# Gate chunks of a ConvFFN by seven block products, with deferred epilogues and a second sum of squares

## Chip, core and metric

One core of a Trainium2 chip runs the whole program in one launch. The metric is device time in microseconds: the median of repeated runs, with the lowest and the highest beside it. One further run is profiled, and all rows below come from that one execution.

## What is computed

A small two-layer decoder trunk (model width 1024; 544 tokens, 512 of a prompt and 32 of samples, in two halves of 272 columns). Layer 0 is RMSNorm, a gated recurrent block, and a ConvFFN; layer 1 is shared K/V, dilated attention, and a second ConvFFN. The change lies nearly all in the two ConvFFNs, and a little in the first RMSNorm:

```python
D_MODEL, D_FF = 1024, 3072
def rmsnorm(x, g):
    return x * lax.rsqrt(jnp.mean(x * x, axis=-1, keepdims=True) + EPS) * g

def causal_dwconv(prev, x, w, b):                  # width 3 here
    xc = jnp.concatenate([prev, x], axis=1)
    return b + sum(xc[:, j:j + T] * w[j] for j in range(3)), xc[:, T:]

def conv_ffn(h, prev, w_up, conv_w, conv_b, w_down):
    g, v = jnp.split(h @ w_up, 2, axis=-1)         # gates and values, 3072 each
    gc, new_prev = causal_dwconv(prev, g, conv_w, conv_b)
    return (jax.nn.gelu(gc) * v) @ w_down, new_prev

x = x + conv_ffn(rmsnorm(x, g_f), ...)
```

## The kernel before

**Layout.** Activations lie transposed: a tile of 128 channels by 2 halves of 272 tokens. `X[0..7]` is the residual stream. A matmul works on an fp32 operand split into a high part (`hh`, `HH`, weights' `hi`) and a remainder (`hl`, `HL`, `lo`); each product of a 128x128 weight block with 272 columns is three matmuls: hi·hi, hi·lo, lo·hi (`step3`, L192). An output chunk of 128 channels over 8 input chunks and 2 halves is 48 matmuls; a pair of chunks is 96.

**Weights.** They come in units of 512 KB into `raw` (three buffers). A unit is split into two `w` tiles (eight buffers): ScalarE (ACT) copies the high part (L131, L142, L163, 128x1024 each; L148, 128x512), VectorE (DVE) subtracts it (L132, L143, L164, L149). `conv_more(room)` issues these as far ahead as `w` tiles are to be had, in the order of the list `items`; `use()` calls it before each new weight.

**Seven block products.** A pair of value chunks (`duo`, `product`, L485) is not made as 96 matmuls. The weight blocks and the token halves form 2x2 block matrices, and seven products of 12 matmuls each give the four results, with sums of weights (DVE, 128x512 each: L155, L156, L158, L159) and of inputs (`T12`, `T34`, made once per layer) as operands: 84 matmuls. The products accumulate in one-bank PSUM tiles (`bank`). ACT copies partial results out (`snap`, L490; L585), DVE adds them (L587) into `cr` in SBUF.

**Order in an FFN.** There are 24 gate chunks and 24 value chunks, in six groups j of four. In each group: four gate chunks, each `full_job` (48 matmuls into a two-bank PSUM tile `big`), after each of them `g_done`; then `down(j-1)`, eight output chunks o of 24 matmuls each (two `big` tiles in turn), each added into `X[o]` by DVE (L610); then two value pairs, after each of them `v_done`. The sixth `down` stands behind the loop. So from group 1 on one round of the loop is 192 + 192 + 168 = 552 matmuls, and there are five such rounds in each of two FFNs.

`g_done` works on a gate chunk: DVE multiplies it by `rstd` into `E` (L532, L534), ACT and DVE do the width-3 convolution (L540, L541, L543, L546), ACT the gelu (L549), and GpSimd (POOL) multiplies by `rstd` once more (L550). `v_done` multiplies value and gate (DVE L553) and splits the result into `HH` and `HL` (ACT L295, DVE L296).

**PSUM.** `psum_pools(bigs, banks)` closes the PSUM pools and opens new ones: three `big` and two `bank` outside the FFN loops, two and four inside. A tile of a new pool waits for the readers of what lay at its place.

**The first norm.** While the inputs arrive, squares of `X[k]` are made on ACT (odd k, L262) or DVE (even k, L264) into two buffers `sqx`; POOL adds seven of them into `ss` (L266). `total` sums over partitions by a matmul with ones (L271), in the midst of the first three output chunks, and makes `rstd` from it.

**Order of instructions.** TensorE (PE) takes its matmuls in the order written. For the other engines a scheduler decides the order within a window; each engine then works in that order.

Of the kernel before, what the change touches and what calls it, by code (L numbers as in the profile page):

```python
# [14 lines left out]
P = 128  # L15
# [30 lines left out]
def trunk_kernel(ctx, tc, wall, xin, par_d, cst_d, msk_d, rope_d, bmask_d, ckT_d, cv_d,  # L46
# [20 lines left out]
    def psum_pools(bigs, banks):  # L67

        if psum:
            psum["ctx"].close()  # L70
        psum["ctx"] = ExitStack()
        for name, n in (("pp", bigs), ("aux", banks)):
            psum["n"] = psum.get("n", 0) + 1
            psum[name] = psum["ctx"].enter_context(pool(f"{name}{psum['n']}", n, space=bass.MemoryType.PSUM))
# [14 lines left out]
    def ffn_items(b0):  # L89
        def up(kind, j, i):  # L90
            return b0 + (0 if j == 0 else 12 * j - 4) + 4 * kind + i

        def duo(kind, j, i):
            return [("a", n, up(kind, j, i), up(kind, j, i + 1)) for n in range(4)]

        def down(j):
            return [("u", b0 + (16 + 12 * j if j < 5 else 68) + q) for q in range(4)]

        order = []
        for j in range(6):  # L100
            order += [("u", up(0, j, i)) for i in range(4)] + (down(j - 1) if j else []) + duo(1, j, 0) + duo(1, j, 2)
        return order + down(5)
# [77 lines left out]
    def use(held=0):  # L180

        conv_more(WBUFS - held)
        i = nxt["use"]
        nxt["use"] += 1
        return split.pop(items[i][1] if items[i][0] == "u" else i)
# [56 lines left out]
    class Norm:  # L242
# [12 lines left out]

        def square(self, k, on_act=True):
            if k == 0:
                sq = self.ss = self.hp.tile([P, 2, T], F32, name="ss", tag="ss", bufs=1)
            else:
                sq = self.hp.tile([P, 2, T], F32, name="sqx", tag="sqx", bufs=2)  # L260
            if on_act:
                ACT.activation(sq, X[k], AF.Square)  # L262
            else:
                DVE.tensor_tensor(sq, X[k], X[k], op=ALU.mult)  # L264
            if k:
                POOL.tensor_tensor(self.ss, self.ss, sq, op=ALU.add)  # L266

        def total(self):
            ps = [bank(), bank()]
            for h in range(2):  # L270
                PE.matmul(ps[h][:, :T], lhsT=ones, rhs=self.ss[:, h, :], start=True, stop=True)  # L271
            tc.keep_in_program_order(ACT.preload_act_table_set("natural_log_exp_and_others"))
# [148 lines left out]
    for k in range(KC):  # L421
        if k in (0, 4):
            for u in range(3):
                conv(u, k * P, k * P + HALF)
        nrm.gain(k, pcol("g_a", k))
        nrm.square(k, on_act=k % 2 == 1)
    first = [(split.pop(u), big()) for u in range(3)]
# [36 lines left out]

    def product(form, snap, done):

# [26 lines left out]
        prod(0, A, True)  # L493
        s1 = keep(A)
        prod(1, G, True)
        p5 = keep(G)
        prod(2, A, False)
        u2 = keep(A)
        B = bank()[:, :T]
        prod(3, B, True)  # L500
        done(0, 0, (s1, B))
        prod(4, A, False)
        done(1, 1, (p5, keep(A)))
        prod(5, G, False)
        done(0, 1, (u2, G))
        prod(6, A, False)
        done(1, 0, (A,))

    def ffn(layer, nrm, hpool, fctx, ectx, after):
# [4 lines left out]
        fo = fp.tile([P, FC, 18], F32, name="fo")  # L514
        psum_pools(2, 4)
        E = [fp.tile([P, 562], F32, name=f"E{i}") for i in range(2)]
# [10 lines left out]
        def g_done(c, src):  # L527
# [46 lines left out]
        def form(n, k, part):  # L574
            x0, x1 = nrm.x(2 * k)[part], nrm.x(2 * k + 1)[part]
            t12, t34 = T12[k][part], (T34h, T34l)[part][k]
            return {0: x0[:, 0], 1: t12[:, 0], 2: t12[:, 1], 3: x1[:, 0], 4: t34[:, 0], 5: x1[:, 1], 6: t34[:, 1]}[n]

        def duo(c):
# [9 lines left out]
            product(form, snap, done)  # L589
            return t  # L590

        def gates(j):
            for c in range(4 * j, 4 * j + 4):
                g_done(c, full_job(nrm.x))

        def values(c):
            for i, t in enumerate(duo(c)):
                v_done(c + i, t)

# [4 lines left out]
        def down(j):  # L604
            for q in range(4):
                w = use()
                for o in (2 * q, 2 * q + 1):
                    ps = big()
                    down_part(o, ps, w, j, range(4))
                    DVE.tensor_tensor(X[o], X[o], ps[:, :, :T], op=ALU.add)  # L610

        def down_last():
# [25 lines left out]
        for c in (2, 3):  # L638
            g_done(c, full_job(nrm.x))
        for j in range(6):  # L640
            if j:
                gates(j)
                down(j - 1)
            values(4 * j)
            values(4 * j + 2)
        SP.dma_start(ffn_d[:, layer], fo)
        ectx.close()
# [664 lines left out]
```

## Time and profile before

| | |
|---|---|
| median of 3 runs | 1324.05 us (1323.76 to 1325.4) |
| profiled execution | 1323.6 us |
| its span, first to last instruction | 1321.8 us |
| mean granted TensorE clock over the span | 0.988 |
| PE busy / DVE / ACT / POOL | 96% / 70% / 48% / 19% of the span |

The span is what all the rows below divide up; 1.8 us of the profiled execution lie outside of it. Busy shares are means over stages that are unlike: the stretches in which PE is not busy lie at the start, between the parts, and in attention.

### The profile page before, as it was taken

The page shows a single profiled execution, that of the slowest core. Times are in us where ns is not written, and L with a number is a line of the kernel's source. Part 1 is how long each engine was busy: PE and PEld are TensorE (multiplying, and loading weights), DVE is VectorE, ACT ScalarE, POOL GpSimd, SP SyncE. Part 2 cuts the span into 40 slices and gives each one's busy share as a digit, 9 for nine tenths or more (in the row PEclk, how much of TensorE's full clock was granted, in tenths as well). Part 3 has the DMA queues.
Part 4 walks back from the last instruction along what each step waited for, and adds up shares of the span by engine and source line. Part 5 has one row for each costly group of instructions (what it writes and reads, how often), then busy time and mean ns, then how long its engine had stood idle before and what let it go on. Part 6 is the DMA issues. An engine that isn't in the chain of part 4 may idle for free.

```text
span 1321.8 us, 24032 instructions
## 1 busy us (share of the span) xinstructions
PE 1272.7 (96%) x9853; PEld 1239.3 (94%) x9853; DVE 923.1 (70%) x1429; ACT 628.6 (48%) x1047; POOL 249.8 (19%) x284
## 2 busy tenths in 40 slices
PE   6999989999999999999999998798999999999998
PEld 6999989999999999999999787488999999999998
DVE  7986769766766666667877445779776666666763
ACT  5768646525353434445545255256535343434431
POOL 4464333010101010104114221033110101010100
PEclk8999999999999999999999999898999999999999
DMA  6232221314132322323255252311313232222312
GB/s 204 81 97 97 84 80 33 128 65 128 64 113 81 111 82 89 103 76 140 73 155 173 72 198 104 116 65 33 128 65 112 80 112 81 90 96 74 116 64 84
DMA packets 42174, 130.45 MB, mean 99 GB/s; under 512 B 7792, under 2 KB 8304, under 8 KB 41616
## 3 DMA queue, kind: packets, MB, share of 16 engines
q1 hardware_dynamic: 42064, 128.92, 29.3%
q8 instruction: 77, 1.26, 0.4%
q14 instruction: 33, 0.27, 0.1%
HBM read 119.99 MB, written 8.39 MB: 97 GB/s over the span
## 4 chain that ended last, share of the span: by engine, by line
PE 82%; DVE 10%; ACT 4%; issue 2%; DMA 1%; POOL 0%; SPq 0%; DVEq 0%; ACTq 0%; POOLq 0%
PE big L192 54%; PE bank L485 19%; PE big L881 2%; PE big L817 2%; DVE w L132 1%; PE big L867 1%; ACT w L131 1%; DVE hl L253 1%; DVE cc L358 1%; PE big L962 1%; PE big L714 1%; PE big L930 1%; DMA X<-in_xin 1%; PE bank L1059 0%; PE bank L817 0%
## 5 line engine op out<-in xcount | busy, mean ns | idle before, releaser
L192 PE MATMUL big<-hh,w 128*128 128x272 f32 x2560 | 439.9, 292 | 19.1 <-ACT hh L252 5.9
L192 PEld LDWEIGHTS big<-hh,w 128*128 128x128 f32 x2560 | 368.6, 191 | 20.5 <-ACT hh L252 5.9
L192 PE MATMUL big<-hl,w 128*128 128x272 f32 x1280 | 269.0, 291 | 1.7 <-DVE hl L253 1.6
L192 PE MATMUL big<-HH,w 128*128 128x272 f32 x1536 | 257.2, 288 | 1.0 <-ACT cr L585 1.0
L131 ACT ACTIVATE w<-raw 128x1024 fp32r<-128x1024 f32 (+1 forms) x151 | 156.9, 1039 | 163.5 <-PE big L192 130.6
L192 PEld LDWEIGHTS big<-HH,w 128*128 128x128 f32 x1536 | 217.4, 188 | 1.4 <-ACT cr L585 1.4
L132 DVE TENSOR_TENSOR w<-raw,w 128x1024 fp32r<-128x1024 f32 (+1 forms) x151 | 189.5, 1256 | 29.7 <-PE bank L485 18.8
L192 PEld LDWEIGHTS big<-hl,w 128*128 128x128 f32 x1280 | 203.8, 191 | 2.9 <-DVE hl L253 2.9
L550 POOL TENSOR_TENSOR G<-G,rstd 128x544 f32<-128x544 f32 x48 | 72.4, 1511 | 626.6 <-ACT G L549 626.6
L192 PE MATMUL big<-HL,w 128*128 128x272 f32 x768 | 159.2, 288 | 0.0
L192 PEld LDWEIGHTS big<-HL,w 128*128 128x128 f32 x768 | 120.6, 188 | 0.0
L485 PE MATMUL bank<-hh,w 128*128 128x272 f32 x576 | 119.8, 288 | 0.0
L610 DVE TENSOR_TENSOR X<-X,big 128x544 f32<-128x544 f32 x80 | 57.3, 717 | 64.7 <-PE big L192 64.7
L163 ACT ACTIVATE w<-sum 128x1024 fp32r<-128x1024 f32 x48 | 50.7, 1059 | 104.0 <-PE big L192 102.4
L485 PEld LDWEIGHTS bank<-hh,w 128*128 128x128 f32 x576 | 94.8, 188 | 0.0
L485 PE MATMUL bank<-hl,w 128*128 128x272 f32 x288 | 82.8, 288 | 0.0
L485 PE MATMUL bank<-t34h,w 128*128 128x272 f32 x384 | 80.0, 288 | 0.0
L532 DVE TENSOR_TENSOR E<-big,rstd 128x512 f32<-128x512 f32 x48 | 33.1, 689 | 65.4 <-PE big L192 65.2
L485 PE MATMUL bank<-t12h,w 128*128 128x272 f32 x384 | 76.0, 287 | 0.0
L549 ACT ACTIVATE G<-G 128x544 f32<-128x544 f32 x48 | 31.7, 659 | 93.1 <-DVE G L546 52.2
L266 POOL TENSOR_TENSOR ss<-ss,sqx 128x544 f32<-128x544 f32 x28 | 48.2, 1723 | 115.6 <-ACT sqx L262 112.0
L164 DVE TENSOR_TENSOR w<-sum,w 128x1024 fp32r<-128x1024 f32 x48 | 59.3, 1235 | 12.3 <-PE bank L485 8.8
(266 smaller groups left out, 2099.8 us busy)
## 6 DMA issues: line engine op xcount, KB each, us to landing
raw<-in_wall SPq DMA_DIRECT2D x193, 512.0 KB, 3.5
ck<-in_ckT SPq DMA_DIRECT2D x8, 512.0 KB, 6.3
X<-in_xin SPq DMA_DIRECT2D x8, 272.0 KB, 6.3
out_y<-X SPq DMA_DIRECT2D x8, 272.0 KB, 2.1
cv<-in_cv SPq DMA_DIRECT2D x8, 256.0 KB, 4.1
cvt<-in_cv SPq DMA_DIRECT2D x4, 512.0 KB, 4.2
raw<-in_wall SPq DMA_DIRECT2D x6, 256.0 KB, 5.7
out_kT<-KT SPq DMA_DIRECT2D x1, 1088.0 KB, 5.2
```

Of the source, the lines that this page charges most:

```text
L131: ACT.activation(hi[:, c0:c1], st, AF.Copy)
L132: DVE.tensor_tensor(lo[:, c0:c1], st, hi[:, c0:c1].bitcast(F32), op=ALU.subtract)
L163: ACT.activation(hi, flat, AF.Copy)
L164: DVE.tensor_tensor(lo, flat, hi.bitcast(F32), op=ALU.subtract)
L192: PE.matmul(ps[:, h, :T], lhsT=w[wi], rhs=x[xi][:, h, :], start=first and wi == 0 and xi == 0, stop=last and wi == 1)
L266: POOL.tensor_tensor(self.ss, self.ss, sq, op=ALU.add)
L485: PE.matmul(dst, lhsT=w, rhs=form(n, k, xi), start=first and k == 0 and wi == 0 and xi == 0, stop=k == 3 and wi == 1, skip_group_check=True)
L532: DVE.tensor_tensor(e[:, 2:514].rearrange("p (h t) -> p h t", h=2), prompt(src), prompt(nrm.rstd), op=ALU.mult)
L549: ACT.activation(g, g, AF.Gelu_apprx_tanh)
L550: POOL.tensor_tensor(g, g, nrm.rstd, op=ALU.mult)
L610: DVE.tensor_tensor(X[o], X[o], ps[:, :, :T], op=ALU.add)
L817: PE.matmul(o, lhsT=l, rhs=w[wi][:, 512 * kk:512 * kk + 512], start=k == 0 and wi == 0 and xi == 0, stop=k == KC - 1 and wi == 1)
```

## The change

1. The gate chunks of groups 1 to 5 are made by the seven block products too (`gates_of`, `duo`), with the list `items` altered to match; those of group 0 stay as they are.
2. `g_done` and `v_done` of a pair are put into a list `posts` and traced inside the next `product` (two places) or behind the first two output chunks of `down`. `product` also calls `conv_more` at fixed places with a fixed room.
3. The multiplication of the gelu by `rstd` goes from POOL to DVE.
4. `psum_pools(2, 4)` moves from the start of `ffn` to behind group 0's four gate chunks, and the two pools are laid out in the other order.
5. In the first norm odd squares from k = 3 on are added into a second sum `ss2` by DVE; POOL keeps the even ones. `total` multiplies both with ones.

```diff
         for j in range(6):
-            order += [("u", up(0, j, i)) for i in range(4)] + (down(j - 1) if j else []) + duo(1, j, 0) + duo(1, j, 2)
+            order += duo(0, j, 0) + duo(0, j, 2) + down(j - 1) if j else [("u", up(0, j, i)) for i in range(4)]
+            order += duo(1, j, 0) + duo(1, j, 2)
...
-            if k:
+            if two and k > 1 and k % 2:
+                DVE.tensor_tensor(self.ss2, self.ss2, sq, op=ALU.add)
+            elif k and sq is not self.ss2:
                 POOL.tensor_tensor(self.ss, self.ss, sq, op=ALU.add)
...
-                PE.matmul(ps[h][:, :T], lhsT=ones, rhs=self.ss[:, h, :], start=True, stop=True)
+                for x in (self.ss, self.ss2):
+                    if x is not None:
+                        PE.matmul(ps[h][:, :T], lhsT=ones, rhs=x[:, h, :], start=x is self.ss,
+                                  stop=x is self.ss2 or self.ss2 is None)
...
         prod(1, G, True)
         p5 = keep(G)
+        conv_more(WBUFS - 4)
         prod(2, A, False)
         u2 = keep(A)
+        if posts:
+            posts.pop(0)()
+        conv_more(WBUFS - 2)
         B = bank()[:, :T]
         prod(3, B, True)
         done(0, 0, (s1, B))
+        conv_more(WBUFS)
         prod(4, A, False)
         done(1, 1, (p5, keep(A)))
+        if posts:
+            posts.pop(0)()
+        conv_more(WBUFS - 2)
...
-        psum_pools(2, 4)
...
-            POOL.tensor_tensor(g, g, nrm.rstd, op=ALU.mult)
+            DVE.tensor_tensor(g, g, nrm.rstd, op=ALU.mult)
...
-        def gates(j):
-            for c in range(4 * j, 4 * j + 4):
-                g_done(c, full_job(nrm.x))
+        def gates_of(c):
+            t = duo(c)
+            posts.extend([lambda i=i: g_done(c + i, t[i]) for i in range(2)])
...
                     DVE.tensor_tensor(X[o], X[o], ps[:, :, :T], op=ALU.add)
+                    if posts:
+                        posts.pop(0)()
...
+        psum_pools(2, 4)
         for j in range(6):
             if j:
-                gates(j)
+                gates_of(4 * j)
+                gates_of(4 * j + 2)
                 down(j - 1)
```

**PE, where group 1's gates end and its `down` begins.** Before, the gates write `big` tiles with pairs of matmuls for the two halves:

```order
L192 MATMUL big<-hl,w 128x272 x2
L192 MATMUL big<-hh,w 128x272 x2
L192 MATMUL big<-HH,w 128x272 x2
L192 MATMUL big<-HL,w 128x272 x2
L192 MATMUL big<-HH,w 128x272 x4
```

Now the gates end with a product into a `bank` tile, from the sums of inputs:

```order
L497 MATMUL bank<-t34l,w 128x272
L497 MATMUL bank<-t34h,w 128x272 x2
L497 MATMUL bank<-t34l,w 128x272
L497 MATMUL bank<-t34h,w 128x272
L194 MATMUL big<-HH,w 128x272 x2
L194 MATMUL big<-HL,w 128x272 x2
```

What follows in `down` is the same; what moved is the kind and the number of the matmuls ahead of it.

**DVE, around the start of `down` in a round.** The names `X_77`, `X_81`, `X_85`, `X_88` are the residual tiles 0 to 3; `E_2283`, `E_2284` the two conv buffers. Before (L610 adds an output chunk into `X`):

```order
L132 TENSOR_TENSOR w<-raw,w 128x1024
L541 SCALAR_TENSOR_TENSOR cc<-E_2291,par,cc 128x560
L610 TENSOR_TENSOR X_77<-X_77,big 128x544
L543 SCALAR_TENSOR_TENSOR G<-E_2291,par,cc 128x2x256
L546 SCALAR_TENSOR_TENSOR G<-E_2291,par,cc 128x2x16
L156 TENSOR_TENSOR sum<-sum,raw 128x512
L530 COPY E_2291<-par 128x8x2
L159 TENSOR_TENSOR sum<-raw,sum 128x512
L610 TENSOR_TENSOR X_81<-X_81,big 128x544
L143 TENSOR_TENSOR w<-raw,w 128x1024
L610 TENSOR_TENSOR X_85<-X_85,big 128x544
```

Now, from the last weight split of the gates on (L638 is the same add):

```order
L133 TENSOR_TENSOR w<-raw,w 128x1024
L552 COPY E_2283<-par 128x8x2
L554 TENSOR_TENSOR E_2283<-cr,rstd 128x512
L638 TENSOR_TENSOR X_77<-X_77,big 128x544
L556 TENSOR_TENSOR E_2283<-cr,rstd 128x8x4
L552 COPY E_2284<-par 128x8x2
L554 TENSOR_TENSOR E_2284<-cr,rstd 128x512
L556 TENSOR_TENSOR E_2284<-cr,rstd 128x8x4
L156 TENSOR_TENSOR sum<-raw 128x512
L563 SCALAR_TENSOR_TENSOR cc<-E_2283,par,cc 128x560
L563 SCALAR_TENSOR_TENSOR cc<-E_2284,par,cc 128x560
L565 SCALAR_TENSOR_TENSOR G<-E_2283,par,cc 128x2x256
```

From the row behind these on, with the second of these adds and the third:

```order
L568 SCALAR_TENSOR_TENSOR G<-E_2283,par,cc 128x2x16
L638 TENSOR_TENSOR X_81<-X_81,big 128x544
L565 SCALAR_TENSOR_TENSOR G<-E_2284,par,cc 128x2x256
L572 TENSOR_TENSOR G<-G,rstd 128x544
L568 SCALAR_TENSOR_TENSOR G<-E_2284,par,cc 128x2x16
L144 TENSOR_TENSOR w<-raw,w 128x1024
L572 TENSOR_TENSOR G<-G,rstd 128x544
L638 TENSOR_TENSOR X_85<-X_85,big 128x544
```

The whole epilogue of two gate chunks, which before came chunk by chunk inside the gates, now stands among the first three adds into `X`.

**DVE, in the first norm** (L255 is the split of the inputs, L270 a square, L272 the new sum):

```order
L270 TENSOR_TENSOR sqx<-X_91 128x544
L255 SCALAR_TENSOR_TENSOR hl<-X_94,par,hh 128x544
L272 TENSOR_TENSOR ss_141<-ss_141,sqx 128x544
L255 SCALAR_TENSOR_TENSOR hl<-X_96,par,hh 128x544
L270 TENSOR_TENSOR sqx<-X_96 128x544
L255 SCALAR_TENSOR_TENSOR hl<-X_98,par,hh 128x544
L272 TENSOR_TENSOR ss_141<-ss_141,sqx 128x544
```

Before, these rows stood there without the two sums, the square of `X_96` ahead of its split, and POOL did seven sums; it now does three.

## Rows read from the trace of the kernel before

**Rows 1.** The page: busy time, share of the span and instructions of each engine; below, the granted clock in 40 slices of the span, in tenths.

```profile
PE 1272.7 (96%) x9853; PEld 1239.3 (94%) x9853; DVE 923.1 (70%) x1429; ACT 628.6 (48%) x1047; POOL 249.8 (19%) x284
PEclk8999999999999999999999999898999999999999
```

**Rows 2.** The page: the chain of work that ended last, by engine.

```profile
PE 82%; DVE 10%; ACT 4%; issue 2%; DMA 1%; POOL 0%; SPq 0%; DVEq 0%; ACTq 0%; POOLq 0%
```

**Rows 3.** Stretches of one round each (from the first matmul of a group's gates to that of the next): length, busy time of each engine with its instructions, granted clock, DMA share, GB/s. One of the ten, and the sum and mean of all ten.

```profile
319.29:388.43 69.14, 69.14 (x554) 69.14 (x554) 47.00 (x70) 28.57 (x46) 5.85 (x4) 1.00 0.28 93
...
sum 692.45, PE 692.44 PEld 692.01 DVE 467.86 ACT 285.71 POOL 60.74; mean PE 69.24 PEld 69.20 DVE 46.79 ACT 28.57 POOL 6.07
```

**Rows 4.** The chain of work in the round 319.29 to 388.43, in order of time: start, us, what.

```profile
319.29 48.11 PE big L192 x384
367.40 21.03 PE bank L485 x168
```

**Rows 5.** The same round, instructions by line and form: count, busy us, mean ns of one, idle time before them.

```profile
L132 DVE TENSOR_TENSOR w<-raw,w 128x1024 fp32r<-128x1024 f32 x8 | 9.8, 1223 | 1.9 <-PE bank L485 1.7
L131 ACT ACTIVATE w<-raw 128x1024 fp32r<-128x1024 f32 x8 | 8.5, 1059 | 8.0 <-PE big L192 6.5 <-DMA raw<-in_wall 1.3 <-PE bank L485 0.2
L550 POOL TENSOR_TENSOR G<-G,rstd 128x544 f32<-128x544 f32 x4 | 5.8, 1462 | 63.3 <-ACT G L549 63.3
L490 ACT ACTIVATE snap<-bank 128x272 f32<-128x272 f32 x8 | 3.2, 397 | 4.5 <-PE bank L485 4.4
L553 DVE TENSOR_TENSOR cr<-cr,G 128x544 f32<-128x544 f32 x4 | 2.7, 718 | 0.0
L587 DVE TENSOR_TENSOR cr<-snap,bank 128x272 f32<-128x272 f32 x4 | 1.7, 428 | 0.0
```

**Rows 6.** DVE in that round at the start of `down`, in order of time: start, us, instruction. `down` begins at 343.23 (the last row, of PE, from its own order of time).

```profile
344.33 0.68 DVE L532 TENSOR_TENSOR E<-big,rstd 128x512 f32<-128x512 f32 x1
344.93 0.18 DVE L534 TENSOR_TENSOR E<-big,rstd 128x32 f32<-128x32 f32 x1
345.03 1.21 DVE L132 TENSOR_TENSOR w<-raw,w 128x1024 fp32r<-128x1024 f32 x1
346.16 0.79 DVE L541 SCALAR_TENSOR_TENSOR cc<-E,par,cc 128x560 f32<-128x560 f32 x1
346.88 0.71 DVE L610 TENSOR_TENSOR X<-X,big 128x544 f32<-128x544 f32 x1
347.51 0.74 DVE L543 SCALAR_TENSOR_TENSOR G<-E,par,cc 128x512 f32<-128x512 f32 x1
348.17 0.24 DVE L546 SCALAR_TENSOR_TENSOR G<-E,par,cc 128x32 f32<-128x32 f32 x1
348.33 0.68 DVE L156 TENSOR_TENSOR sum<-sum,raw 128x512 f32<-128x512 f32 x1
348.93 0.17 DVE L530 COPY E<-par 128x16 f32<-128x16 f32 x1
...
343.23 0.41 PE L192 MATMUL big<-HH,w 128*128 128x272 f32 x2
```

**Rows 7.** What PE waited for, over the whole span: us in total, times, longest.

```profile
PE bank L271 <- POOL ss L266: 5.6, 1, 5.6
PE big L192 <- DVE E L534: 5.4, 2, 3.0
PE big L192 <- DVE X L1129: 4.2, 1, 4.2
```

**Rows 8.** The start: POOL's seven sums; a split and the last square of DVE; PE's matmuls on the sum and the first behind them.

```profile
9.42 5.54 POOL L266 TENSOR_TENSOR ss<-ss,sqx 128x544 f32<-128x544 f32 x3 [8.38 <-ACT sqx L262]
18.23 7.46 POOL L266 TENSOR_TENSOR ss<-ss,sqx 128x544 f32<-128x544 f32 x4 [3.26 <-DVE sqx L264]
...
18.00 0.77 DVE L253 SCALAR_TENSOR_TENSOR hl<-X,par,hh 128x544 fp32r<-128x544 f32 x1
20.02 0.73 DVE L264 TENSOR_TENSOR sqx<-X 128x544 f32<-128x544 f32 x1 [1.25 <-POOL ss L266]
...
25.73 2.18 PE L271 MATMUL bank<-ss,ones 128*128 128x272 f32 x4 [5.59 <-POOL ss L266]
27.33 1.04 PE L192 MATMUL big<-hh,w 128*128 128x272 f32 x2
```

**Rows 9.** The start of layer 0's FFN. PE: its first matmul, the first of the third chunk, one 18 matmuls later, and the first product of the values. DVE: the last step of `rstd`. PE clock in 214 to 220 us.

```profile
198.39 0.79 PE L192 MATMUL big<-hh,w 128*128 128x272 f32 x2 [3.56 <-ACT h L564]
215.29 0.79 PE L192 MATMUL big<-hh,w 128*128 128x272 f32 x2 [2.36 <-DVE E L534]
218.77 0.67 PE L192 MATMUL big<-hh,w 128*128 128x272 f32 x4
228.82 0.29 PE L485 MATMUL bank<-hh,w 128*128 128x272 f32 x1
...
213.52 0.72 DVE L283 SCALAR_TENSOR_TENSOR rstd<-sqx,rstd 128x544 f32<-128x544 f32 x1
...
214.00:220.00 6.00, 4.71 (x26) 4.75 (x27) 5.90 (x13) 4.89 (x9) 0.00 (x0) 0.72 0.26 87
```

**Rows 10.** A short wait of PE in layer 0's mixer, and the granted clock around it.

```profile
75.46 0.52 PE L192 MATMUL big<-xfh,w 128*128 128x272 f32 x2 [1.15 <-ACT rg L385]
72.00:77.00 5.00, 3.60 (x27) 3.19 (x26) 4.93 (x9) 4.49 (x6) 3.37 (x8) 1.00 0.28 108
```

More of the change, by code (lines that the diff above doesn't have):

```diff
@@ L71, in psum_pools @@
         psum["ctx"] = ExitStack()
-        for name, n in (("pp", bigs), ("aux", banks)):
+        for name, n in (("aux", banks), ("pp", bigs)):
             psum["n"] = psum.get("n", 0) + 1
@@ L180, in use @@
     def use(held=0):
-        conv_more(WBUFS - held)
+        if items[nxt["use"]][0] == "u" or nxt["conv"] <= nxt["use"]:
+            conv_more(WBUFS - held)
         i = nxt["use"]
@@ L254, in gain, with square @@
             self.hi[k], self.lo[k] = hi, lo
-        def square(self, k, on_act=True):
+        def square(self, k, on_act=True, two=False):
             if k == 0:
                 sq = self.ss = self.hp.tile([P, 2, T], F32, name="ss", tag="ss", bufs=1)
+                self.ss2 = None
+            elif two and k == 1:
+                sq = self.ss2 = self.hp.tile([P, 2, T], F32, name="ss2", tag="epsx", bufs=1)
             else:
@@ L425, in trunk_kernel @@
         nrm.gain(k, pcol("g_a", k))
-        nrm.square(k, on_act=k % 2 == 1)
+        nrm.square(k, on_act=k % 2 == 1, two=True)
     first = [(split.pop(u), big()) for u in range(3)]
@@ L462, in trunk_kernel, with product @@
         nrm.gain(c, pcol("g_f", c))
-    def product(form, snap, done):
+    def product(form, snap, done, posts):
         A, G = bank()[:, :T], bank()[:, :T]
@@ L501, in product @@
         done(0, 0, (s1, B))
+        conv_more(WBUFS)
         prod(4, A, False)
         done(1, 1, (p5, keep(A)))
+        if posts:
+            posts.pop(0)()
+        conv_more(WBUFS - 2)
         prod(5, G, False)
         done(0, 1, (u2, G))
+        conv_more(WBUFS)
         prod(6, A, False)
         done(1, 0, (A,))
+        conv_more(WBUFS)
     def ffn(layer, nrm, hpool, fctx, ectx, after):
@@ L577, in form, with flush @@
             return {0: x0[:, 0], 1: t12[:, 0], 2: t12[:, 1], 3: x1[:, 0], 4: t34[:, 0], 5: x1[:, 1], 6: t34[:, 1]}[n]
+        posts = []
+        def flush(n=2):
+            for _ in range(min(n, len(posts))):
+                posts.pop(0)()
         def duo(c):
@@ L587, in done @@
                     DVE.tensor_tensor(t[i][:, h], *terms, op=ALU.add)
-            product(form, snap, done)
+            product(form, snap, done, posts)
             return t
-        def gates(j):
-            for c in range(4 * j, 4 * j + 4):
-                g_done(c, full_job(nrm.x))
+        def gates_of(c):
+            t = duo(c)
+            posts.extend([lambda i=i: g_done(c + i, t[i]) for i in range(2)])
         def values(c):
-            for i, t in enumerate(duo(c)):
-                v_done(c + i, t)
+            t = duo(c)
+            posts.extend([lambda i=i: v_done(c + i, t[i]) for i in range(2)])
         def down_part(o, ps, w, j, ks):
@@ L610, in down @@
                     DVE.tensor_tensor(X[o], X[o], ps[:, :, :T], op=ALU.add)
+                    if posts:
+                        posts.pop(0)()
         def down_last():
@@ L645, in ffn @@
             values(4 * j + 2)
+        flush()
         SP.dma_start(ffn_d[:, layer], fo)
```

## Prediction

> **What bounds the kernel now.** I read the page first. PE is busy for 96% of the span and the chain that ended last is PE for 82% of it [rows 1, 2], so a change pays if it shortens PE's work or PE's waits. The ten full rounds of the FFNs come next: each lasts 69.1 to 69.4 us, PE is busy in all of it at granted clock 1.00 (2.4 GHz), DVE for 46.8 us (68%), ACT for 28.6 us, DMA for 0.28 [rows 3]. The chain inside such a round is nothing but matmuls: 384 in 48.11 us, which is 0.1253 us each, and 168 in 21.03 us, 0.1252 us each [rows 4]. So a matmul costs the same in a `big` and in a `bank` tile, and nothing else is on the path. The ten rounds make 692.45 us, more than half of the span. What PE waits for outside of them is short and lies in the start and in the first chunks of the FFNs [rows 7].
>
> **Matmuls removed.** A round has 192 matmuls for four gate chunks, 192 in `down`, 168 for the values. Two pairs of gates by seven products are 2 x 84 = 168, so 528 are left, 24 fewer. At 0.1253 us that is 3.0 us a round, 30.1 us over ten. The new length without any wait is 66.1 us.
>
> **Work added on the other engines, per pair of gates.** Conversions: before, two units, so two copies of 1024 on ACT and two subtractions of 1024 on DVE. Now 3.5 of each, and four sums of 512 on DVE. With 1.223 us (L132), 1.059 us (L131) and 0.68 us for a sum [rows 5, 6] that is 1.5 x 1.223 + 4 x 0.68 = 4.55 us more on DVE and 1.6 us on ACT. Results: three adds on DVE at 0.428 us, 1.3 us, and five copies on ACT at 0.397 us, 2.0 us. The multiplication by `rstd` moves to DVE: two of 128x544, which I price as L553, 0.718 us, so 1.4 us. In a round DVE gets 2 x 7.3 = 14.6 us more and ACT 2 x 3.6 = 7.2 us. ACT ends at 36 of 66 us and is no bound. DVE ends at 46.8 + 14.6 = 61.4 us, 93% of 66.1. Those are busy times, though, and DVE's instructions overlap at their ends: a split of 1024 is followed by the next after 1.13 us where its row says 1.21, a 512 after 0.60 instead of 0.68 [rows 6]. By starts the sum is nearer 57.6 us, 87%. Either way DVE fits, on average. The loads are the same units in the same number, and DMA has room [rows 3].
>
> **Where DVE is late.** The average isn't even. In the gates of the new order a pair brings DVE 13.9 us by starts (3.5 splits at 1.13, four sums at 0.60, three adds at 0.35, and an epilogue of two chunks: `E` 0.60 + 0.10, copy 0.12, conv 0.72 and 0.66 + 0.16, `rstd` 0.67 each) against 84 x 0.125 = 10.5 us of PE. So DVE falls behind in the gates and has to catch up in `down`, where it has about 10 us of work in 24. What is late next is the add into `X`: it frees the `big` tile, and `down` has two. A chunk is 24 matmuls, 3.0 us. With T the start of `down`, chunk o ends at T + 3.0 (o + 1), and chunk o + 2 needs its tile at T + 3.0 (o + 2): 6.0, 9.0, 12.0. I walk down DVE's new order. The last but one split of the gates starts behind its copy at about T, the `rstd` product and the last split follow, and DVE is at the copy of `E` at about T + 2.8. Then `E` 0.60; the add of chunk 0 ends near T + 4.1, in time for 6.0. Then 0.10, 0.12, 0.60, 0.10, a sum 0.60, two convolution steps 0.72 each, 0.66, 0.12: T + 7.8, and the add of chunk 1 ends near T + 8.5, in time for 9.0 by half a microsecond. Then 0.66, 0.67, 0.12, 1.13, 0.67, and 0.65 for the add itself: T + 12.4, where 12.0 is wanted. With the hand-over PE stands for about 0.7 us; behind it come only single adds and sums, and DVE has caught up. Bounds: nothing, if DVE reaches `down` half a microsecond earlier; 2 us, if it runs at the busy times instead of the starts (about 20 instructions by 0.08) and comes out of the gates late by as much again. I take 0.7. A round then gains 3.0 - 0.7 = 2.3 us, ten gain 23 us.
>
> **Does a stall that short cost clock?** After a wait of 1.15 us in the mixer the clock stayed at 1.00 [rows 10]. After one of 2.36 us it did not: 18 matmuls took 215.29 to 218.77, 3.48 us instead of 18 x 0.125 = 2.25, at a mean clock of 0.72 in that stretch [rows 9]. So 0.7 us costs itself and 2.4 us costs 1.2 more. The Trainium skill, page "TensorE: Matmul & The Clock Gate", section on the clock gate in Part 1, has it that the throttled clock is the default and activity lifts it, so a kernel with gaps starts each piece slowly. By that rule applied to every gap, each round would pay the 1.2 us as well and the ten would gain 11 us, not 23; the row after the 1.15 us wait speaks against it for a gap this short.
>
> **POOL's part.** POOL's multiplications by `rstd` (1.46 us each) are hidden now [rows 5] and nobody waits for them in a round, so taking them off gains nothing by itself; their cost on DVE is in the sum above.
>
> **The start.** PE waits 5.59 us for `ss`: POOL makes seven sums, three from 9.42 and four from 18.23 to 25.69, about 1.86 us each, and the last square on DVE waits for POOL too [rows 8]. Now POOL has three and DVE three more at 0.65. From the split at 18.00 on DVE has split 0.70, sum, split, square, split, sum: it ends near 22.7, and POOL's last sum near 23. PE can start 2.7 us earlier, but makes two sums by ones more, which cost 27.33 - 25.73 = 1.6 us for two at the low clock. I take a gain of 1.5 us; bounds 0 (the extra sums eat it) and 3.5.
>
> **The starts of the FFNs.** Without new PSUM pools there the first pair need not wait (3.56 us in layer 0, 4.2 in layer 1), and a third `big` lets the third chunk go without the wait of 2.4 to 3.0 us [rows 7, 9]. But DVE is busy throughout: `rstd` ends at 214.24 whatever PE does. The fourth chunk needs the first one's tile, which is freed near 216.1, so it ends near 222.3. Then the pools change, and the first product waits until DVE has read the fourth chunk, which stands behind two splits, two epilogues, three products by `rstd` and a sum in its order: 216.8 + about 10.5 = 227.3. PE restarts slowly, 1.2 us: as if it had started at 228.5, where it now starts at 228.82. So the waits move behind the fourth chunk and the sum is zero in both layers; bounds -1.5 and +1.5 each.
>
> **The sum.** 1323.6 - 23 - 1.5 - 0 = 1299 us against the profiled execution; the median of before is 0.45 us above it, and I leave that out: 1299 us.
>
> **Rivals.**
> - *No stall.* DVE reaches `down` a little earlier, each round gains 3.0: 1323.6 - 30 - 1.5 = 1292 us. For it: the walk misses by 0.4 us only. Against: the order puts a whole split between the second and third add.
> - *A stall of 1.3 to 2 us a round.* DVE comes out of the gates later, because a sum or split there waits for a `w` tile or a load; 13 to 20 us of the 30 go back: 1305 to 1312 us. For it: DVE at 87 to 93% has little to catch up with. The same price comes another way if the clock falls at every stall, however short: 0.7 + 1.2 = 1.9 us a round, 1311 us; the 1.15 us wait in the mixer speaks against it.
> - *Slower.* One mechanism: the third add into `X` is late by more than the gap that the clock bears. A stall of 2.4 us brings 1.2 us of low clock with it [rows 9], 3.6 us in all against the 3.0 saved: each round is 0.6 us longer and the kernel ends near 1328 us; it decides where the third add ends at about T + 14, which is 1.7 us later than in my walk. For it: 1.7 us is two splits' wait. Against: the walk uses this trace's spacings, and DVE has half of `down` free behind that add.
> - *No change.* The 24 matmuls go and PE waits for DVE as long as they took, with no clock lost: 3.0 us of stall spread over places, 1322 us. The same clock row speaks against an exact balance.
>
> **How the numbers follow.** My forecast (stall 0.4 to 1.2) 0.50, no stall 0.17, longer stall 0.17 (0.04 of it by the clock at short stalls), no change 0.04, slower 0.12. The range from 1288 to 1313 takes in the first three with their bounds (the start to 3.5, the FFN starts to 3): 0.84. A measurement of this kernel tells about 0.2%, 2.6 us, from no change. Faster by more than that are the first three cases, 0.84; slower 0.12; the same 0.04.
>
> **What would show it.** In a round's stretch: 66.8 us, 528 matmuls, DVE near 60 us busy, POOL near nothing. In PE's waits: a new row on DVE's L638, ten times, below 1.2 us each, at the third add. At the start: the wait for `ss` near 3 us. At the FFN starts: no wait of the first pair and the third chunk, and one of about 5 us for L556 ahead of the first product. The prediction is wrong if PE waits inside the products (for a split, a `snap` or a `bank`), which I put at nothing, or if the clock in the rounds falls below 1.00.

## Result and the profile after

The changed kernel takes 1292.54 us (median; 1292.44 to 1292.59) against 1324.15 us of the kernel before (1323.76 to 1325.4) on the same chip: a ratio of 0.976, 95% interval 0.9743 to 0.9777. That is 31.6 us less, where 25 us less was forecast; the time lies in the range, between the forecast and the rival without a stall.

The page of the profile after: busy time of each engine, the granted clock in 40 slices, the chain that ended last by engine.

```profile
PE 1242.0 (96%) x9617; PEld 1207.0 (94%) x9617; DVE 1028.2 (80%) x1660; ACT 690.7 (54%) x1187; POOL 172.2 (13%) x232
PEclk9999999999999999999999999899899999999999
PE 71%; DVE 19%; ACT 4%; issue 3%; DMA 1%; POOL 1%; SPq 0%; POOLq 0%; DVEq 0%; ACTq 0%
```

Against [rows 1] PE is busy for 31 us less and DVE for 105 us more, and DVE now holds 19% of the chain where it held 10% [rows 2]. A whole round, here from the values of one group to the end of `down` that follows the next group's gates, reads so (length, busy PE, weight loads, DVE, ACT, POOL, clock, DMA share, GB/s; one in each layer, and the sum of all eight such rounds):

```profile
291.20:357.71 66.51, 66.49 (x530) 66.27 (x529) 57.71 (x92) 34.78 (x61) 0.00 (x0) 1.00 0.31 96
974.22:1040.70 66.48, 66.42 (x530) 66.20 (x529) 57.73 (x92) 34.75 (x60) 0.00 (x0) 1.00 0.30 96
sum 532.25, PE 531.59 PEld 529.85 DVE 461.36 ACT 278.31 POOL 0.00; mean PE 66.45 PEld 66.23 DVE 57.67 ACT 34.79 POOL 0.00
```

The mean is 532.25 / 8 = 66.53 us where it was 69.24 [rows 3]. DVE is busy for 87% of it, ACT for 52%. Two pieces make up a round:

```profile
266.78:291.20 24.42, 24.35 (x194) 24.13 (x193) 21.73 (x37) 7.97 (x15) 0.00 (x0) 1.00 0.24 74
291.20:333.25 42.05, 42.05 (x338) 42.05 (x337) 35.98 (x56) 26.80 (x47) 0.00 (x0) 1.00 0.36 110
```

The second is two value pairs and two gate pairs, 336 matmuls in 42.05 us or 0.1252 us each: PE waits for nothing in any product. The first is `down`: 192 matmuls would be 24.05 us and it takes 24.42, so it holds the whole loss of a round, a third of a microsecond. The chain of that round says what it is (start, us, what; from the second add into `X` on):

```profile
274.50 0.63 DVE X L638
275.13 0.66 DVE G L565
275.80 0.63 DVE G L572
276.43 0.16 DVE G L568
276.59 1.14 DVE w L144
277.73 0.64 DVE G L572
278.36 0.64 DVE X L638
279.01 0.04 issue
279.05 12.31 PE big L194 x96
```

That is the third add of the prediction's walk, and these are the rows that it named. What PE waited for, over the whole span:

```profile
PE bank L497 <- DVE E L556: 9.5, 2, 4.7
PE big L194 <- DVE E L556: 4.0, 2, 2.9
PE bank L281 <- POOL ss L274: 1.8, 2, 1.1
PE big L194 <- DVE X L1162: 0.7, 1, 0.7
PE big L194 <- DVE X L638: 0.3, 1, 0.3
```

Against [rows 7], the wait for the sum of squares has shrunk from 5.6 to 1.1 us, those of the FFNs' first pairs are nearly gone (4.2 to 0.7 us in layer 1), and a new one of 4.7 us stands in each layer in front of the first product. The wait for the first evacuations is 4.0 us in both layers together, where it was 5.4; it is the fourth chunk's now and not the third's. The stall at the third add is in this list for one round only; in the others it is too short for it.

Set beside each other, the starts of the same work in the two traces tell where the 31.4 us of span went:

| mark | before | after | earlier by |
|---|---|---|---|
| product with ones, first norm | 25.73 | 22.02 | 3.7 |
| first value product, layer 0 | 228.82 | 222.35 | 6.5 |
| first `down`, layer 0 | 274.05 | 266.78 | 7.3 |
| fifth `down`, layer 0 | 550.79 | 532.72 | 18.1 |
| last `down`, layer 0 | 596.48 | 578.86 | 17.6 |
| first value product, layer 1 | 925.24 | 905.64 | 19.6 |
| first `down`, layer 1 | 970.48 | 949.78 | 20.7 |
| fifth `down`, layer 1 | 1247.72 | 1216.01 | 31.7 |
| last `down`, layer 1 | 1293.59 | 1262.22 | 31.4 |

### The profile page after: what moved, and what is told of

Its sections match the earlier page's. It is cut to its first block, busy times and chain, and to the rows that moved or that the text cites. A ratio compares the mean times of both kernels' runs of the same rounds, so it can differ in the third digit from the quotient of the medians.

```text
span 1290.4 us, 23770 instructions
## 1 busy us (share of the span) xinstructions
PE 1242.0 (96%) x9617; PEld 1207.0 (94%) x9617; DVE 1028.2 (80%) x1660; ACT 690.7 (54%) x1187; POOL 172.2 (13%) x232
## 3 DMA queue, kind: packets, MB, share of 16 engines
q1 hardware_dynamic: 42064, 128.92, 31.4%
## 4 chain that ended last, share of the span: by engine, by line
PE 71%; DVE 19%; ACT 4%; issue 3%; DMA 1%; POOL 1%; SPq 0%; POOLq 0%; DVEq 0%; ACTq 0%
PE big L194 32%; PE bank L497 29%; DVE w L133 3%; PE big L914 2%; DVE cc L563 2%; PE big L850 2%; DVE G L565 1%; DVE G L572 1%; DVE E L554 1%; DVE X L638 1%; PE big L900 1%; DVE hl L255 1%; DVE cc L369 1%; ACT w L132 1%; DVE w L144 1%
## 5 line engine op out<-in xcount | busy, mean ns | idle before, releaser
L194 PE MATMUL big<-hh,w 128*128 128x272 f32 x1280 | 220.6, 291 | 11.3 <-ACT hh L254 6.1
L497 PE MATMUL bank<-hh,w 128*128 128x272 f32 x1056 | 222.3, 290 | 9.5 <-DVE E L556 9.5
L194 PEld LDWEIGHTS big<-hh,w 128*128 128x128 f32 x1280 | 184.2, 190 | 12.4 <-ACT hh L254 6.1
L497 PEld LDWEIGHTS bank<-hh,w 128*128 128x128 f32 x1056 | 175.8, 190 | 9.8 <-ACT G L571 9.8
L194 PE MATMUL big<-hl,w 128*128 128x272 f32 x640 | 133.8, 290 | 1.7 <-DVE hl L255 1.6
L497 PEld LDWEIGHTS bank<-t34h,w 128*128 128x128 f32 x704 | 116.0, 188 | 0.0
L497 PEld LDWEIGHTS bank<-t12h,w 128*128 128x128 f32 x704 | 114.6, 191 | 0.0
L194 PEld LDWEIGHTS big<-hl,w 128*128 128x128 f32 x640 | 101.3, 190 | 2.7 <-DVE hl L255 2.7
L497 PE MATMUL bank<-t12l,w 128*128 128x272 f32 x352 | 101.9, 290 | 0.0
L497 PE MATMUL bank<-t34l,w 128*128 128x272 f32 x352 | 101.4, 288 | 0.0
```

Of the source, the lines that this page charges most:

```text
L194: PE.matmul(ps[:, h, :T], lhsT=w[wi], rhs=x[xi][:, h, :], start=first and wi == 0 and xi == 0, stop=last and wi == 1)
L497: PE.matmul(dst, lhsT=w, rhs=form(n, k, xi), start=first and k == 0 and wi == 0 and xi == 0, stop=k == 3 and wi == 1, skip_group_check=True)
```

## Experiments

The theory after the result (A in what follows): a round gains what the 24 matmuls cost, less the stand at the third add; the start gains by the second sum; the new PSUM layout only moves waits; and DVE has next to nothing to spare between the gates and the third add. The rivals are that part of the gain belongs to the other edits, and that DVE does have room. Each ratio is to the kernel before on the same chip.

**The gates by full jobs again, all else kept.**

```diff
-                gates_of(4 * j)
-                gates_of(4 * j + 2)
+                for c in range(4 * j, 4 * j + 4):
+                    flush(1)
+                    g_done(c, full_job(nrm.x))
```

(with the list `items` as before to match)

> The changed kernel, but the gates of groups 1 to 5 are full jobs of 48 matmuls into a big tile again, each with its epilogue right behind; the values' remaining work is still traced later, and the multiplication by rstd stays on DVE. Theory A: the gain of a round is the 24 matmuls, so a round is 69.2 us again instead of 66.5 and ten of them cost 27 to 30 us: 1320 to 1322 us. Rival B: part of the gain is the order and the move off POOL, which stay: 1310 us or less.

1320.87 us, ratio 0.9978 (0.9968 to 0.9987). One round in its trace:

```profile
338.68:408.00 69.32, 69.32 (x555) 69.32 (x554) 48.93 (x75) 28.46 (x47) 0.00 (x0) 1.00 0.29 92
```

The round is as long as before; theory A holds. Of the whole change, 28 us hang on the seven products, and the other edits alone are worth 3 us.

**One sum of squares again.**

```diff
-        nrm.square(k, on_act=k % 2 == 1, two=True)
+        nrm.square(k, on_act=k % 2 == 1)
```

> The changed kernel, but with all seven sums of squares of the first norm on POOL again. Theory A: the second sum is worth what the start shows, the product with ones at 22.02 us instead of 25.73, so 3.7 to 4.1 us are lost: 1296 to 1297 us, with PE's wait for the sum near 5.6 us again and nothing else moved. Rival B: the start is given back behind it, because the mixer now waits for DVE (0.5 to 0.9 us at four places that had no such wait before): at most 2 us are lost, 1294 us.

1296.99 us, ratio 0.9794 (0.9781 to 0.9808): 4.5 us slower than the changed kernel. The product with ones stands at 25.54 us, and PE waits 5.6 us for it. Theory A; the mixer gives nothing back.

**PSUM laid out at the start of the FFN again.**

```diff
         fo = fp.tile([P, FC, 18], F32, name="fo")
+        psum_pools(2, 4)
...
-        psum_pools(2, 4)
         for j in range(6):
```

> The changed kernel, but the PSUM pools are laid out anew at the start of each FFN as before. Theory A (as predicted): the waits only move, from the first product to the first pair and the third chunk, and the slow clock with them; within 1.5 us of 1292.5. Rival B: the first product's place in the trace (6.5 us earlier in layer 0, of which 4.1 come from the start; 1.5 us earlier in layer 1) tells the worth, so 3 to 4 us are lost: 1296 us. In both: no wait of 4.7 us of the first product any more, and waits of 3 to 4 us of the first pair instead.

1291.61 us, ratio 0.9756 (0.9743 to 0.9769): 0.9 us less than the changed kernel, with intervals that overlap. The waits of PE in it:

```profile
PE big L194 <- DVE E L557: 4.3, 2, 2.2
PE big L194 <- DVE X L1162: 4.2, 1, 4.2
PE big L194 <- ACT h L587: 3.6, 1, 3.6
```

These are the waits of [rows 7, 9] again, and the first product waits no more. The new place is worth nothing by itself, as forecast.

**The multiplication by `rstd` on POOL again.**

```diff
-            DVE.tensor_tensor(g, g, nrm.rstd, op=ALU.mult)
+            POOL.tensor_tensor(g, g, nrm.rstd, op=ALU.mult)
```

> The changed kernel, but the multiplication of the gelu by rstd is on POOL again. Theory A: DVE is what the third add of a round waits for, and two products of 0.64 us stand ahead of that add; without them the add is early and the 0.25 to 0.35 us that each round stands there are gone: 1290 us, POOL near 72 us busier. Rival B: POOL's work slows DVE's (1.71 instead of 1.23 us for one split in the kernel before, while POOL multiplied), which eats it: 1292 to 1294 us. Rival C: the gelu comes too late for the values: over 1296 us.

1319.1 us, ratio 0.9965 (0.9951 to 0.9978): 26 us slower than the changed kernel. Neither A nor B had that; C had the sign but not the place, since PE waits for adds into `X` and not for the values' gates. Its largest wait of PE and two of its rounds:

```profile
PE big L194 <- DVE X L638: 19.6, 30, 1.2
...
295.24:364.29 69.05, 66.99 (x531) 66.37 (x529) 59.23 (x88) 34.64 (x61) 7.95 (x4) 1.00 0.28 92
364.29:433.31 69.02, 67.00 (x531) 66.36 (x530) 59.22 (x88) 34.64 (x61) 7.95 (x4) 1.00 0.28 92
```

DVE has four instructions fewer in a round (x88 for x92) and is busy longer, 59.2 us for 57.7. The reason stands in the order of time around `down`; POOL's multiplications first, then instructions of DVE that started beside them:

```profile
263.65 1.39 POOL L572 TENSOR_TENSOR G<-G,rstd 128x544 f32<-128x544 f32 x1 [33.64 <-ACT G L571]
269.28 3.64 POOL L572 TENSOR_TENSOR G<-G,rstd 128x544 f32<-128x544 f32 x1 [4.24 <-ACT G L571]
...
263.72 1.91 DVE L563 SCALAR_TENSOR_TENSOR cc<-E,par,cc 128x560 f32<-128x560 f32 x1
271.60 1.37 DVE L556 TENSOR_TENSOR E<-cr,rstd 128x32 f32<-128x32 f32 x1
277.79 0.96 DVE L568 SCALAR_TENSOR_TENSOR G<-E,par,cc 128x32 f32<-128x32 f32 x1
279.81 1.83 DVE L156 TENSOR_TENSOR sum<-raw 128x512 f32<-128x512 f32 x1
281.56 0.71 DVE L638 TENSOR_TENSOR X<-X,big 128x544 f32<-128x544 f32 x1
```

In the changed kernel the first four of these DVE instructions take 0.79, 0.18, 0.24 and 0.68 us. Each of the four multiplications on POOL holds one instruction of DVE for 0.7 to 1.2 us, more than the 0.64 us that it costs DVE to do the work itself. None of the four ends before POOL's multiplication beside it has: the one of 128x32 ends at 271.60 + 1.37 = 272.97, POOL's at 269.28 + 3.64 = 272.92. All four fall ahead of the third add, two of them between the second and the third. That add starts at 281.56 - 268.39 = 13.2 us into `down`, where it started at 278.28 - 266.78 = 11.5 us; and three adds of a round are late instead of one. DVE's order is another one here too, since the scheduler made it anew; the next run keeps it.

**A multiplication on POOL that nobody reads, beside the one on DVE.** This tells the held-up DVE from a product that merely comes late.

```diff
             DVE.tensor_tensor(g, g, nrm.rstd, op=ALU.mult)
+            idle = fp.tile([P, 2, T], F32, name="idle", tag="idle", bufs=1)
+            POOL.tensor_tensor(idle, g, nrm.rstd, op=ALU.mult)
```

> The changed kernel, with one more multiplication of 128x544 on POOL behind each gate chunk's own on DVE; its result goes into a tile that nobody reads. Theory A: POOL's work itself holds DVE up. In the run with the multiplication on POOL one DVE instruction beside each of them took about 1.1 us longer (a convolution step 1.91 us instead of 0.79, a sum 1.83 instead of 0.68), and down grew by 2.5 us a round. Here the same, though nobody waits for POOL: 1315 to 1325 us, with PE waiting for adds into X. Rival B: the loss in that run came from the late product, not from the port; then nothing is lost here: 1293 us.

1320.66 us, ratio 0.9976 (0.9967 to 0.9985), and PE waits where it did in the run above:

```profile
PE big L194 <- DVE X L640: 18.6, 30, 1.1
...
295.00:364.00 69.00, 67.14 (x531) 66.49 (x530) 61.04 (x92) 34.69 (x61) 8.34 (x4) 1.00 0.28 92
...
271.15 2.23 POOL L574 TENSOR_TENSOR idle<-G,rstd 128x544 f32<-128x544 f32 x1 [5.23 <-DVE G L572]
272.06 1.34 DVE L552 COPY E<-par 128x16 f32<-128x16 f32 x1
```

Nobody waits for this work, and it costs 28 us: DVE has the changed kernel's 92 instructions in a round and needs 61.0 us for them, not 57.7. Over the whole trace DVE's 1660 instructions stand in the same order as in the changed kernel, so the order isn't the cause either. The copy shown took 0.17 us there. The loss comes from POOL's working, not from its result.

**The kernel before with that multiplication on DVE.**

```diff
-            POOL.tensor_tensor(g, g, nrm.rstd, op=ALU.mult)
+            DVE.tensor_tensor(g, g, nrm.rstd, op=ALU.mult)
```

> The kernel before, with the multiplication of the gelu by rstd on DVE instead of POOL and nothing else. Theory A: DVE is idle 2 us ahead of each evacuation there, so nobody sees the difference in the rounds: within 2 us of the kernel before, DVE's busy time about the same (48 times 0.7 us more, less what POOL held up). Rival B: this move alone is a good part of the gain: 1310 us or less.

1323.75 us, ratio 0.9997 (0.9988 to 1.0006). In the kernel before DVE sat idle ahead of 32 of its 48 evacuations (L532), 65.2 us in all, so what POOL took of its time was free. POOL took less there, too: beside its 48 multiplications 20 DVE instructions were held, for 0.19 us a multiplication on average, where the kernel with the changed order and the multiplication on POOL had 46 and 0.99 us. Theory A: the move is worth nothing there and 26 us here.

**Work traced at once.**

```diff
-            posts.extend([lambda i=i: g_done(c + i, t[i]) for i in range(2)])
+            for i in range(2):
+                g_done(c + i, t[i])
```

(and the same in `values`)

> The changed kernel, but a pair's remaining work is traced right behind its own product, not inside the next. Theory A: the scheduler's window moves it nearly as far by itself; by its order the second add of a round stands behind one more convolution step (0.82 us), where its margin was half a microsecond, so 0.3 us a round: 1293 to 1296 us. Rival B: tracing it later is what lets DVE keep up; without it PE waits in the products too, over 1 us a round: 1303 us or more.

1299.72 us, ratio 0.9816 (0.9803 to 0.983): 7.2 us slower. The second add, theory A's place, is not late: `down` takes 24.1 us there, less than in the changed kernel. PE waits inside the products, as rival B had it, but less than B's price:

```profile
PE bank L497 <- ACT snap L502: 7.4, 10, 1.0
...
291.50:334.50 43.00, 42.28 (x338) 42.06 (x337) 37.14 (x58) 26.74 (x48) 0.00 (x0) 1.00 0.30 101
```

ACT's copies of partial products come late, once in each of ten rounds, and the four pairs take 43.0 us for 42.05. Two of these copies stand behind the first convolution steps of both chunks, at 326.50; in the changed kernel the first of the two comes ahead of them, at 324.50. So the deferral is worth 7 us, and it is ACT's order that it mends.

**More work for DVE.** One convolution step of each gate chunk (L565, 0.66 us) done twice, to the same result.

```diff
             DVE.scalar_tensor_tensor(prompt(g), e[:, 2:514].rearrange("p (h t) -> p h t", h=2), wcol_(2),
                                      cc[:, 0:512].rearrange("p (h t) -> p h t", h=2), op0=ALU.mult, op1=ALU.add)
+            DVE.scalar_tensor_tensor(prompt(g), e[:, 2:514].rearrange("p (h t) -> p h t", h=2), wcol_(2),
+                                     cc[:, 0:512].rearrange("p (h t) -> p h t", h=2), op0=ALU.mult, op1=ALU.add)
```

> The changed kernel with one convolution step of each gate chunk (128x512 on DVE, 0.66 us by starts) done twice, to the same result: 2.6 us more of DVE in a round of 66.5 us. Theory A: DVE has no spare time between the gates and the third add of down, so the repeats ahead of it lengthen PE's wait there from 0.25 us to about 2 us: ten rounds lose 17 to 20 us, 1310 to 1313 us, with the clock in the rounds still 1.00. Rival B: the same wait also costs the clock, 1.2 us each: 1322 to 1325 us. Rival C: DVE has the 8 us spare that its busy share of 88% suggests, and nothing is lost: 1293 us.

1320.69 us (1314.94 to 1323.99), ratio 0.9966 (0.9951 to 0.9981). Its waits, and `down` in five rounds:

```profile
PE big L194 <- DVE X L640: 21.0, 10, 2.3
...
268.66:296.71 28.05, 25.88 (x195) 25.66 (x193) 24.43 (x42) 8.42 (x15) 0.00 (x0) 0.94 0.21 72
338.76:365.26 26.50, 24.46 (x195) 24.25 (x193) 24.27 (x42) 8.31 (x15) 0.00 (x0) 1.00 0.22 73
407.31:433.75 26.44, 24.36 (x195) 24.13 (x193) 24.26 (x42) 8.31 (x15) 0.00 (x0) 1.00 0.20 71
963.72:990.38 26.66, 24.40 (x195) 24.18 (x194) 24.47 (x42) 8.30 (x15) 0.00 (x0) 1.00 0.22 76
1237.85:1265.83 27.98, 25.92 (x195) 25.71 (x193) 24.19 (x40) 8.30 (x15) 0.00 (x0) 0.94 0.21 78
```

2.6 us of work on an engine that is busy for 87% cost 2.1 us a round: nearly all of it comes out at the third add. On that theory A holds and rival C falls. The clock is between A and B: eight of the ten waits leave it at 1.00, two take it down, and those two rounds lose another 1.5 us each. The time misses A's 1310 to 1313 us by 8. In the profiled execution (1318.03 us) the clock of the two rounds and 2.7 us more of waiting in front of the first products are what A had left out; over the ten executions the time rises from 1314.94 to 1323.99 us as the mean granted clock falls from 0.987 to 0.982.

**PSUM tiles that wait one by one.** With the pools' waits by tile the first product waits only for what lay in its own banks.

```diff
-        if space:
-            kw["space"] = space
-        else:
-            kw["reuse_waits"] = "tile"
+        kw["reuse_waits"] = "tile"
+        if space:
+            kw["space"] = space
```

> The changed kernel, but tiles of a new PSUM pool wait tile by tile for what lay at their place, not all for the last reader. By the program the first product then waits no longer for the fourth gate chunk's evacuation. Theory A: the wait of 4.7 us goes in both layers and the slow clock behind it (2 us each), at most 13 us; DVE, which is busy there, gives part of it back: 1282 to 1287 us. Rival B: DVE is the bound of that stretch, PE waits inside the products for splits and adds instead: 1290 to 1293 us.

1288.23 us, ratio 0.9725 (0.9713 to 0.9738): 4 to 5 us less than the changed kernel. The wait of 4.7 us is gone in both layers, and a part of it comes back as waits for `snap` in the first products:

```profile
PE bank L496 <- ACT snap L501: 4.7, 3, 2.9
```

It lies between the two expectations; PE starts the values at 217.55 and is then held by the engines behind it.

**The same, and the epilogues in `down` one output chunk later.**

```diff
-                    if posts:
+                    if posts and o in (1, 2):
                         posts.pop(0)()
```

> As psum_tile, and the two epilogues in down are traced behind its second and third output chunk instead of the first and second, so that the third add into X stands 0.8 us earlier in DVE's order. Theory A: the stand of 0.25 to 0.35 us in each of ten rounds goes as well, 3 us below psum_tile. Rival B: the epilogue comes later and something behind it (the values' gates) waits instead: no gain.

1284.36 us, ratio 0.9702 (0.9689 to 0.9714), 4 us less. `down` takes 24.07 to 24.20 us in all ten rounds: the stall at the third add is gone, as theory A has it.

**The same, and POOL's subtractions for the sums of inputs on DVE**, in `make_forms`:

```diff
-                POOL.tensor_tensor(h1[:, 0], h2[:, 1], h1[:, 1], op=ALU.subtract)
-                POOL.tensor_tensor(h1[:, 1], h2[:, 0], t[:, 1], op=ALU.subtract)
+                DVE.tensor_tensor(h1[:, 0], h2[:, 1], h1[:, 1], op=ALU.subtract)
+                DVE.tensor_tensor(h1[:, 1], h2[:, 0], t[:, 1], op=ALU.subtract)
```

> As tile_late, and the 16 subtractions that POOL does for the sums of inputs at the starts of the FFNs are on DVE. Theory A: DVE is the bound of that stretch (busy throughout in the trace), and a POOL subtraction of about 1.1 us holds DVE up by more than its own 0.35 us on DVE, so rstd and the first evacuations come 2 to 5 us earlier in each layer: 1276 to 1282 us against 1284 of tile_late. Rival B: they are 0.35 us more each on the engine that is the bound: 1286 to 1290 us.

1281.56 us, ratio 0.9685 (0.9672 to 0.9698): inside theory A's times, with the smallest gain that it had. The intervals of this run and the last overlap.

**The same, and the other norms' sums of squares on DVE:**

```diff
             elif k and sq is not self.ss2:
-                POOL.tensor_tensor(self.ss, self.ss, sq, op=ALU.add)
+                (POOL if two else DVE).tensor_tensor(self.ss, self.ss, sq, op=ALU.add)
```

> As tile_forms, and the sums of squares of all norms but the first are on DVE too (7 sums of 0.65 us each instead of POOL's 1.5 to 1.9 us). Theory A: the same exchange once more, a further 1 to 4 us gained. Rival B: DVE has no room ahead of the total, and each sum is 0.65 us on the path: 2 to 8 us lost against tile_forms.

1276.85 us, ratio 0.965 (0.9637 to 0.9664): theory A again, a little over its 4 us, and 15 us better than the changed kernel. Whether the shorter sums or the DVE instructions that POOL no longer holds made these last two gains, the runs don't separate. A round of the last kernel:

```profile
284.63:350.80 66.17, 66.17 (x531) 66.17 (x530) 57.65 (x92) 34.77 (x61) 0.00 (x0) 1.00 0.30 96
```

PE is busy for all of it, and 66.17 us is 528 matmuls at 0.1253 us. The rounds are at their floor for that many matmuls; what is left lies at the start, in attention and where the FFNs begin.

## Why the prediction was right, and where it was off

**Matmuls removed: right.** 42.05 us for the 336 products of a round, 3.0 us less than before, and the run with full gates gives 69.3 us back.

**DVE's load: right by starts.** The sum by starts was 57.6 us, and the trace has 57.7. The other sum, 61.4, added full durations to a busy time in which overlapping ends count once; a window's busy time is to be compared with spacings, not with mean durations.

**The stall: right place, half the size.** The walk put the adds' ends at T + 4.1, 8.5 and 12.4. They ended at 3.9, 8.3 and 12.1; DVE in the changed kernel, four rows with `down` starting at 266.78:

```profile
269.37 0.17 DVE L552 COPY E<-par 128x16 f32<-128x16 f32 x1
270.05 0.71 DVE L638 TENSOR_TENSOR X<-X,big 128x544 f32<-128x544 f32 x1
274.42 0.72 DVE L638 TENSOR_TENSOR X<-X,big 128x544 f32<-128x544 f32 x1
278.28 0.71 DVE L638 TENSOR_TENSOR X<-X,big 128x544 f32<-128x544 f32 x1
```

DVE was at the first copy at T + 2.6, not 2.8; from there on the walk is right to 0.1 us. To the 0.4 us that the walk then gave I added 0.3 for the hand-over, which the chain shows as 0.04. The stall is a third of a microsecond, not 0.7, and the row on L638 that was to stand ten times in PE's waits stands there once. Eight whole rounds gained 69.24 - 66.53 = 2.7 us each, not 2.3, and ten of them some 27, not 23.

**The start: mis-sized.** Forecast 1.5 us, at most 3.5; the product with ones comes 3.7 us earlier, and undoing the edit costs 4.5. The sum was expected near 23, behind POOL's last addition, and came at 22.02. The walk on DVE ended near its 22.7, at 22.54, by luck: its terms add up to 22.05, its six instructions began at 16.22 and not at 18.00, and two of them, beside POOL's additions, took 1.88 and 1.84 us instead of 0.77 and 0.71. Wrong was also the price of the two added products, 1.6 us, taken from [rows 8], where PE had waited 5.59 us and the granted clock was 0.50 from 25.73 to 30.00:

```profile
22.02 2.23 PE L281 MATMUL bank<-ss,ones 128*128 128x272 f32 x8 [1.10 <-POOL ss L274]
23.88 0.62 PE L194 MATMUL big<-hh,w 128*128 128x272 f32 x2
```

Eight records take 1.86 us here, where four took 1.6. Behind the wait of 1.10 us the granted clock is 1.00 from 22.02 to 27.00, as the prediction itself had read it after a like wait in [rows 10]; I didn't carry that to this place. So the low clock behind the long wait, which goes with that wait, was left out of the gain.

**The starts of the FFNs: right in sum.** The first product came after a wait of 4.74 us (5.0 forecast). The slow clock behind it cost 2.3 us: 222.35 to 266.78 is 44.4 us for 42.1 us of matmuls; 1.2 was forecast. The undone layout is 0.9 us faster, inside the bounds of plus and minus 1.5 a layer. With it the sum closes: 27 us of the rounds and 4.5 of the start, less 0.9, is 30.6 of the 31.6.

**POOL's part: true of the kernel before, not asked for the changed one.** The prediction said that taking the multiplications off POOL gains nothing by itself. In the kernel before that is so. In the changed order it decides nearly the whole gain: with them on POOL the kernel is at 0.9965. So the 28 us of the seven products and the 26 us of this move are not two parts of a sum; each needs the other. The row was there ([rows 5], 1462 ns), and so was the sign of it in the trace before, where a split that takes 1.22 us at other places stood beside such a multiplication (349.19 to 350.97):

```profile
350.34 1.71 DVE L143 TENSOR_TENSOR w<-raw,w 128x1024 fp32r<-128x1024 f32 x1
```

I read it as a price that nobody pays, and did not ask who pays it once DVE has no idle time. It did no harm to the time forecast only because the change makes the move; that was luck. The Trainium skill, page "GPSIMD Engine Reference", section "Specifications", has it that GpSimd's SBUF interfaces are shared with VectorE and that they contend with DVE instructions that read two SBUF inputs or run in a 2-port performance mode. The traces agree on the inputs: the four held instructions of the run with the multiplication on POOL read two, and of 41 DVE instructions with an input from PSUM that started beside these multiplications in the three traces that have them none was held. The copy of 128x16 (L552) reads one and was held all the same; in which mode it ran, no row shows.

**The rivals.** The kernel lies at the rival without a stall (1292) by its time, but a stall is there, and the start made up for it. The mechanism of the rivals with a longer stall is real, though this kernel is 2 us away from it: with the third add made late by about 2 us (the repeated step), or the adds by POOL, 26 to 28 of the 31.6 us are gone. The low clock that the slower rival put behind every such stall came in two of ten rounds of the first and in none of the second.

## What to carry to other kernels

When a change fills DVE, price again what POOL does beside it: 48 multiplications on POOL that were free beside a DVE with idle time cost 26 us beside a busy one, and moving them onto the busy engine was the cheaper way. Look for the first place at which the filled engine's late result frees a buffer, and walk its new order up to there by spacings; the mean busy share says nothing about that place. Check at every new layout of PSUM what the first tile waits for.

## What the runs showed of the hardware

- One fp32 multiplication of 128x544 on POOL can hold a DVE instruction that starts beside it, however small: 128x32 took 1.37 us instead of 0.18. With the multiplications on POOL in the changed order, 46 DVE instructions were held beside 48 of them, by 0.56 to 1.20 us. In the traces of that run, the idle product and the kernel before, no held instruction ended before POOL's multiplication; it ended behind it by a time that goes with its own size: 0.05 us for 128x32, 0.55 for 128x512, 1.08 for 128x1024. So its own work waited until POOL was done.
- POOL's multiplication can stretch as well, from 1.39 to 3.64 us. In the longest one shown DVE began two instructions beside it that took their usual time (a product at 269.86, a split at 270.46), before the third was held at 271.60.
- Waits of nearly the same length did not have the same effect on the clock. In the run with the repeated step the ten waits of 2.0 to 2.3 us left the granted clock at 1.00 in eight rounds and brought the mean of the stretch of `down` to 0.94 in two, after waits of 2.17 and 2.06 us, while one of 2.26 us did nothing. Much shorter ones can stand ahead of a low clock, too: in the mixer the changed kernel and the run with PSUM laid out at the start of the FFN both have waits of 0.69, 0.87 and 0.66 us between 38 and 42 us, and then one runs on at 1.00 and the other at 0.51 (the first row is the changed kernel's). What tells them apart was not tried.

```profile
41.40:44.90 3.50, 3.06 (x22) 2.84 (x23) 3.50 (x6) 3.47 (x4) 0.54 (x3) 1.00 0.64 176
41.40:44.90 3.50, 3.31 (x14) 3.31 (x15) 3.50 (x6) 3.47 (x4) 0.53 (x3) 0.51 0.62 176
```
